# The last stage of a one-core encoder layer in two token pairs instead of four token groups at once

## The chip, the cores and the metric

The kernel runs on one core of a Trainium2 chip. Its metric is the time on the device in microseconds (us). Engines are named as the profile names them: PE (TensorE, with PEld for its weight loads), DVE (VectorE), ACT (ScalarE), POOL (GpSimd), SP (SyncE); a "q" behind a name is the engine's instruction queue, from which DMAs are issued. PSUM is the memory that PE writes, in banks of 128 x 512 float32; SBUF is the memory of everything else.

## What is computed

One encoder layer on 512 tokens of width 1024: three gated token mixers, a layer norm, a mixture of 16 experts in which each expert chooses 64 tokens, and a second layer norm. The change touches only the last expert and the second norm:

```python
def expert_choice_ffn(x, w_router, w_gate_up, w_down):
    B, T, D = x.shape
    cap = EC_CAPACITY_FACTOR * T // N_EXPERTS          # 2 * 512 // 16 = 64
    ...
    gate, idx = lax.top_k(jnp.swapaxes(aff, 1, 2), cap)
    xs = x[bidx, idx]
    h = jnp.einsum('becd,edf->becf', xs, w_gate_up)
    hg, hu = jnp.split(h, 2, axis=-1)
    ye = jnp.einsum('becf,efd->becd', jax.nn.silu(hg) * hu, w_down)
    ye = ye * gate[..., None].astype(ye.dtype)
    return jnp.zeros_like(x).at[bidx, idx].add(ye)

    ffn = expert_choice_ffn(x, w_router[l], w_gate_up[l], w_down[l])
    x = layer_norm(DN_ALPHA * x + ffn, ln2_g[l], ln2_b[l])
```

The layer norm takes mean and variance over the 1024 columns of a token, and gives (x - mean) / sqrt(var + 1e-5) * g + b.

## The kernel before, in words

**Experts.** The weights of the 16 experts stream through a ring of SBUF tiles on SP's queue (`ring`, issues at L829, some 2 MB or 1 MB a transfer). For each expert e, `gate_up` (L1312) makes two products, `act_h` the activation, `h_transpose` (L1330, copied by DVE at L1335) the transposed h, and `down` (L1347) the product with the down weights, y, 64 tokens x 1024 columns. `down` then splits y into a rounded high part and a remainder: `hi_lo`, a cast on ACT (L97) and a subtraction on DVE (L98). Two experts share one such pair of tiles (yh, yl), 128 rows. A product with a one-hot matrix GT (128 rows to 128 tokens, `g[:, m]`) scatters them back to tokens; high part and remainder are two matmuls in the rounded type fp32r. The sum over the experts, with the residual, is kept in SBUF as ACC, in four groups of 128 tokens, m = 0 to 3; mp is a pair of groups (0, 1 or 2, 3).

**The order of the work** is that in which the code is written; each engine runs its instructions in that order, and semaphores between engines are put in by the tile framework from the tiles that instructions read and write. PSUM tiles come from banks named by letters: `PB("S", ...)` takes the bank S, and has to wait until the tile that had it is done with. "mm" is a set of banks that rotate.

**The last stage** is `last_down`, called behind `down(14)`. The 1024 output columns of expert 15 are worked in four quarters q of 256 columns, since its weights come in that order, 1 MB for one quarter:

- `preload(q)` (L1443) puts ACC's columns of quarter q, which `split_acc` has split into high part and remainder, into PSUM by an identity matmul, one bank for each pair, so that the additions can accumulate onto them. Quarter 1 is preloaded earlier; quarter 2 is preloaded between the first two products, quarter 3 behind addition 2. Quarter 0 has none: DVE adds it to ACC (L1514).
- `product(q)` (L1467): 16 fp32 matmuls of expert 15's h with the weights of the quarter (in the profile 32, as each fp32 matmul is two). The output is 64 tokens x 256 columns, put as two halves of 128 columns (o = 0 on partitions 0 to 63, o = 1 on 64 to 127). All four quarters write one PSUM bank, the tile `yq`, in columns of their own.
- `split(q)`: `hi_lo` for each half, on ACT and DVE (L97, L98, 64 x 128).
- `add(q)` (L1480): eight fp32r matmuls, four groups by (yh, yl).
- statistics: `bn_stats` on DVE, for each group and quarter (L1484, L1516), and `bn_aggr` for each group at the end (L1538).
- `scaled(q)`: ACT copies the sums from PSUM to ACC (L1492), POOL multiplies them by g of the norm (L1488). The last quarter is done by DVE in one step, from PSUM (L1497).

**The norm.** g·(x - mean)·r + b, with r = 1/sqrt(var + eps), is formed as x·g·r plus a product of rank 13. `ch` (128 tokens x 4 groups x 13) holds, for each token, 1, -mean, 1/r and -mean·r in high parts and remainders; its rows come from a chain of small operations: ACT's root (L1540), DVE L1541 to L1548 and L1551 to L1553, POOL L1549 and L1550. r itself is y: a reciprocal and a Newton step. `ch` is transposed on PE for each group (rowT, L1558), copied to SBUF by ACT (`rows`, L1560), and multiplied with the rows of g and b (`low_rank`, L1566). Two matmuls of the identity (L1562) stand between transposes and low ranks. For the columns 0 to 511 (h = 0) `put` (L1504) brings x·g into PSUM by an identity matmul, the low rank is added there, and ACT scales by r (L1573). For the columns 512 to 1023 (h = 1) the low rank stands alone in PSUM, and DVE makes x·g·r plus low rank (L1571). Each (m, h) is then stored, 256 KB: six stores on SP's queue, and those of (2, 0) and (3, 0) on ACT's (L1574).

Of the kernel before, what the change touches and what calls it, by code (L numbers as in the profile page):

```python
# [69 lines left out]
def layer_kernel(ctx: ExitStack, tc: tile.TileContext, xt, xn, first0, wu, bgate, rpb, gains, wrt,  # L70
# [696 lines left out]
    class Attn:  # L767
# [4 lines left out]
        def add(self, us):  # L772
            self.units += us
# [228 lines left out]
    eps = small([P, 1], "eps", bufs=1)  # L1002
    nc.gpsimd.memset(eps, LN_EPS)
    warm_s = small([P, 1], "warm_s", bufs=1)
# [433 lines left out]
    def preload(q, banks):  # L1438
        t = ACCP.pop(q)
        r = [PB(b, f"xq{q}{mp}", (P, 2, 256)) if isinstance(b, str) else b for mp, b in enumerate(banks)]  # L1440
        for mp in range(2):
            for n in range(2):
                nc.tensor.matmul(r[mp], ident_r, t[:, n, 2 * mp:2 * mp + 2], start=(n == 0), stop=False)  # L1443
        return r

    def last_down(g2, xq, spare):
# [8 lines left out]
        cols = quarters  # L1455
# [15 lines left out]
        def split(q):  # L1471
            b = cols[q].start
            for o in range(2):
                c = slice(b + o * P, b + (o + 1) * P)
                hi_lo(yh[r, c], yl[r, c], part(q, o))

        def add(q):
            order = [(n, m) for m in range(NT) for n in range(2)] if q == 0 else [(n, m) for n in range(2) for m in range(NT)]
            for n, m in order:
                nc.tensor.matmul(xq[q][m // 2][:, m % 2], g[:, m], (yh, yl)[n][:, cols[q]], start=(q == 0 and n == 0),  # L1480
                                 stop=(n == 1 and (q == 0 or m % 2 == 1)))

        def stats(q, m):
            nc.vector.bn_stats(st[:, m, q], xq[q][m // 2][:, m % 2])  # L1484

        def times_g(mp, q):
            x = ACC[mp][:, :, cols[q]]
            nc.gpsimd.tensor_tensor(x, x, g2[:, None, cols[q]].to_broadcast([P, 2, 256]), op=ALU.mult)  # L1488

        def scaled(q):  # L1490
            for mp in range(2):
                nc.scalar.copy(ACC[mp][:, :, cols[q]], xq[q][mp])  # L1492
                times_g(mp, q)

        def scaled_last(q):
            for mp in range(2):
                nc.vector.tensor_tensor(ACC[mp][:, :, cols[q]], xq[q][mp],  # L1497
                                        g2[:, None, cols[q]].to_broadcast([P, 2, 256]), op=ALU.mult)
# [6 lines left out]

        product(0)
        split(0)
        xq[2] = preload(2, (spare.rearrange("p (a b) -> p a b", a=2), "Y"))
        product(1)
        split(1)  # L1510
        add(0)
        for mp in range(2):
            x = ACC[mp][:, :, cols[0]]
            nc.vector.tensor_tensor(x, x, xq[0][mp], op=ALU.add)  # L1514
            for m in (2 * mp, 2 * mp + 1):
                nc.vector.bn_stats(st[:, m, 0], acc_of(m)[:, cols[0]])  # L1516
            times_g(mp, 0)
        product(2)
        split(2)
        add(1)  # L1520
        for m in range(NT):
            stats(1, m)
        scaled(1)
        product(3)
        add(2)
        xq[3] = preload(3, ("T", "S"))
        split(3)
        for m in range(NT):
            stats(2, m)
        add(3)  # L1530
        scaled(2)
        put(0, "mm")
        put(1, "mm")
        put(2, "S")
        put(3, "T")
        for m in range(NT):
            stats(3, m)
            nc.vector.bn_aggr(mv[:, m], st[:, m])  # L1538
        mean, var = mv[:, :, 0], mv[:, :, 1]
        nc.scalar.activation(sg, var, AF.Sqrt, bias=eps)  # L1540
        nc.vector.tensor_scalar(hv, var, LN_EPS, -0.5, op0=ALU.add, op1=ALU.mult)  # L1541
        nc.vector.tensor_scalar(ch[:, :, 3:12:8], mean[:, :, None].to_broadcast([P, NT, 2]), -1.0, None, op0=ALU.mult)
        nc.vector.scalar_tensor_tensor(ch[:, :, 5], mean, -1.0, ch[:, :, 3].bitcast(F32), op0=ALU.mult, op1=ALU.subtract)
        nc.vector.reciprocal(y, sg)
        nc.vector.tensor_tensor(a, y, y, op=ALU.mult)
        nc.vector.tensor_tensor(a, a, hv, op=ALU.mult)
        nc.vector.scalar_tensor_tensor(y, a, 1.5, y, op0=ALU.add, op1=ALU.mult)
        nc.vector.scalar_tensor_tensor(sg, hv, -2.0, y, op0=ALU.mult, op1=ALU.mult)  # L1548
        nc.gpsimd.tensor_copy(ch[:, :, 4:13:8], sg[:, :, None].to_broadcast([P, NT, 2]))  # L1549
# [7 lines left out]
        for m in range(NT):  # L1557
            nc.tensor.transpose(tp[:13, m], ch[:, m].bitcast(F32), ident)  # L1558
# [245 lines left out]
```

## Time and profile before

| | |
|---|---|
| median of 3 runs | 966.16 us (965.75 to 966.56) |
| profiled execution | 966.82 us, span of the profile 965.0 us |
| busy share of the span | PE 98%, PEld 63%, DVE 47%, ACT 29%, POOL 9% |
| last weight transfers | end near 942 us |
| last products of expert 14 | 932.95 to 934.89 us |
| products of expert 15 | start at 935.55, 938.81, 942.07 and 945.89 us |
| root (ACT) | 953.20 us |
| first store issued | 957.43 us |

Times inside the execution are counted from the start of the span. A row of the timeline reads: start, length (both us), engine, line, operation, tile written <- tiles read, shapes, count, and in brackets how long the engine had stood idle and what ended that. A row of the chain of waits reads: start, length, what. In the stretches, each engine's busy time is followed by its count of instructions; then come the clock that PE was granted (1.00 is full speed), the busy share of the DMA engines, and GB/s. In the groups of the page, the numbers behind the bar are the busy time of the group in us and the mean of one instruction in ns. Busy shares of PE include waiting inside a pipelined group, and ends of matmuls are modelled.

### The profile page before, as it was taken

How to read it: one execution, taken by the hardware profiler on the slowest of the kernel's cores; microseconds unless marked ns; L12 is line 12 of the kernel's file. 1: busy time of each engine (PE TensorE's matmuls, PEld its weight loads, DVE VectorE, ACT ScalarE, POOL GpSimd, SP SyncE). 2: the span in 40 equal slices, each digit the busy share in tenths (PEclk: the TensorE clock that was granted, in tenths of full speed). 3: DMA queues.
4: the chain of work that ended last, by engine and by line, in shares of the span. 5: the costliest groups of instructions: out<-in, count | busy, mean ns of one | idle time of the engine just before them, and what ended most of it. 6: DMA issues, size and time to landing. Idle time of an engine off the chain costs nothing.

```text
span 965.0 us, 12910 instructions
## 1 busy us (share of the span) xinstructions
PE 942.6 (98%) x5262; PEld 608.4 (63%) x5262; DVE 453.4 (47%) x851; ACT 276.5 (29%) x539; POOL 84.2 (9%) x98
## 2 busy tenths in 40 slices
PE   9999999999999999999999999999999999998996
PEld 9899878888888888887885333433344333432344
DVE  6347668874376566237454122653322223231426
ACT  6334454543444454223242111100010000100123
POOL 0002303000112231000023000000000000000003
PEclk9999999999999999999999999999999999999998
DMA  9311111111433322564919999999999999999992
GB/s 361 114 67 67 66 66 44 66 58 54 115 91 106 99 83 87 218 266 192 393 43 387 430 418 431 428 432 429 431 429 431 430 431 431 430 430 432 427 410 91
DMA packets 39192, 251.17 MB, mean 260 GB/s; under 512 B 13007, under 2 KB 13391, under 8 KB 24926
## 3 DMA queue, kind: packets, MB, share of 16 engines
q1 hardware_dynamic: 38414, 249.74, 63.8%
q8 instruction: 41, 0.67, 0.3%
q10 hardware_dynamic: 720, 0.62, 0.2%
q14 instruction: 17, 0.14, 0.0%
HBM read 247.46 MB, written 2.10 MB: 259 GB/s over the span
## 4 chain that ended last, share of the span: by engine, by line
PE 79%; DMA 10%; DVE 6%; ACT 2%; issue 2%; POOL 1%; ACTq 0%; DVEq 0%; POOLq 0%; SPq 0%
DMA w<-in_wx 10%; PE g L1312 10%; PE u L1312 9%; PE y L1347 8%; PE gate L282 4%; PE gate L284 4%; PE gate L283 4%; PE gy L670 2%; PE ga L1272 2%; PE pr L282 2%; PE nqk L284 2%; PE nqk L282 2%; PE nqk L283 2%; PE gt L657 1%; PE pr L283 1%
## 5 line engine op out<-in xcount | busy, mean ns | idle before, releaser
L1312 PE MATMUL g<-w,xs 128*64 128x512 f32 x512 | 135.0, 606 | 2.9 <-DMA w<-in_wx 2.9
L1312 PE MATMUL u<-w,xs 128*64 128x512 f32 x512 | 131.6, 592 | 0.0
L1347 PE MATMUL y<-w,hT 128*64 128x512 f32 x480 | 106.6, 594 | 3.3 <-DMA w<-in_wx 2.6
L98 DVE TENSOR_TENSOR y<-y,y 64x512 fp32r<-64x512 f32 x30 | 20.7, 689 | 134.4 <-ACT y L97 134.4
L1312 PEld LDWEIGHTS u<-w,xs 128*64 128x64 f32 x512 | 36.8, 137 | 73.1 <-issue 72.3
L97 ACT CAST y<-y 64x512 fp32r<-64x512 f32 x30 | 17.4, 580 | 224.8 <-PE y L1347 213.5
L98 DVE TENSOR_TENSOR los<-raw_twin,whi 128x1024 fp32r<-128x1024 f32 x42 | 53.4, 1272 | 58.2 <-ACT whi L97 58.0
L1347 PEld LDWEIGHTS y<-w,hT 128*64 128x64 f32 x480 | 33.8, 137 | 72.0 <-issue 64.7
L284 PE MATMUL gate<-xh,los 128*128 128x512 f32 x192 | 74.8, 390 | 0.0
L1312 PEld LDWEIGHTS g<-w,xs 128*64 128x64 f32 x512 | 30.7, 136 | 53.9 <-issue 44.8
L282 PE MATMUL gate<-xh,whi 128*128 128x512 f32 x144 | 57.2, 397 | 0.0
L283 PE MATMUL gate<-xl,whi 128*128 128x512 f32 x144 | 56.1, 390 | 0.0
L1419 DVE TENSOR_TENSOR acc<-acc,cb 128x512 f32<-128x512 f32 x56 | 35.6, 684 | 37.8 <-PE cb L1417 37.8
L97 ACT CAST whi<-raw_twin 128x1024 fp32r<-128x1024 f32 x42 | 44.0, 1049 | 8.2 <-PE wo L1110 4.3
L1488 POOL TENSOR_TENSOR acc<-acc,ln2g 128x512 f32<-128x512 f32 x6 | 7.6, 1276 | 430.1 <-DVE l2s L1516 428.1
L284 PEld LDWEIGHTS gate<-xh,los 128*128 128x128 f32 x192 | 36.0, 188 | 7.7
L98 DVE TENSOR_TENSOR los<-raw_twin,los 128x1024 fp32r<-128x1024 f32 x20 | 25.0, 1249 | 27.0 <-ACT los L97 26.9
L646 ACT ACTIVATE att_twin<-gs,nm 128x512 f32<-128x512 f32 x32 | 21.7, 684 | 49.0 <-DVE nm L645 49.0
L1322 ACT ACTIVATE tg<-g 128x512 f32<-128x512 f32 x16 | 9.5, 597 | 89.2 <-PE g L1312 89.2
L1335 DVE COPY hT<-ht 128x512 f32<-128x512 f32 x15 | 10.4, 691 | 44.4 <-PE ht L1330 44.4
L282 PEld LDWEIGHTS gate<-xh,whi 128*128 128x128 f32 x144 | 27.0, 188 | 6.5 <-issue 1.2
L283 PEld LDWEIGHTS gate<-xl,whi 128*128 128x128 f32 x144 | 27.1, 188 | 5.3
(436 smaller groups left out, 1863.5 us busy)
## 6 DMA issues: line engine op xcount, KB each, us to landing
w<-in_wx SPq DMA_DIRECT2D x83, 2048.0 KB
raw_twin<-in_wu SPq DMA_DIRECT2D x65, 512.0 KB
w<-in_wx SPq DMA_DIRECT2D x26, 1024.0 KB
raw<-in_wu SPq DMA_DIRECT2D x8, 512.0 KB
xr<-in_xt SPq DMA_DIRECT2D x4, 512.0 KB
macc<-in_xn SPq DMA_DIRECT2D x2, 1024.0 KB
first<-in_first SPq DMA_DIRECT2D x4, 384.0 KB
bf<-in_rpb SPq DMA_DIRECT2D x64, 24.0 KB
```

The source lines that it names most:

```text
L97: nc.scalar.copy(hi, src)
L98: nc.vector.tensor_tensor(lo, src, hi.bitcast(F32), op=ALU.subtract)
L282: nc.tensor.matmul(acc, w_h, rh[:, k], start=(k == 0), stop=False)
L283: nc.tensor.matmul(acc, w_h, rl[:, k], start=False, stop=False)
L284: nc.tensor.matmul(acc, w_l, rh[:, k], start=False, stop=(k == nk - 1))
L646: nc.scalar.activation(self.p[:, h], self.s[h], AF.Exp, bias=nm[:, h:h + 1], accum_out=self.sm[:, h:h + 1])
L670: nc.tensor.matmul(self.y[h * 64:h * 64 + 64, :P], ST["vg"][:, kc, kvh * 64:kvh * 64 + 64], self.pt[:, h, kc], start=(kc == 0), stop=(kc = ...
L1272: nc.tensor.matmul(g, XH[:, m, c], oh[:, m, sl], start=(m == 0), stop=False)
L1312: nc.tensor.matmul(GU[e][b][hf * 64:hf * 64 + 64], xs, w[b][:, hf * 512:hf * 512 + 512], start=(k == 0), stop=(k == KD - 1))
L1335: nc.vector.tensor_copy(t, tp)
L1347: nc.tensor.matmul(y[o * 64:o * 64 + 64], hT[:, c, hf * 64:hf * 64 + 64], w[j][:, o * 512:(o + 1) * 512], start=(k == 0 and j == 0), stop= ...
L1419: nc.vector.tensor_tensor(a, a, cb, op=ALU.add)
```

## The change

It touches the last stage and the end of `down(14)` only.

- **Products into two banks.** Quarter q goes into bank S (`yqa`) or Y (`yqb`) by q % 2; of quarter 3, half o = 0 goes into the one and o = 1 into the other. `add(0)` stands behind `product(1)`, `add(1)` directly behind `product(2)`, each in the order of the groups.
- **Quarter 3 isn't split.** ACT and DVE copy one half each, as fp32, into a tile `Y3`, and the addition is one fp32 matmul for each group instead of two fp32r ones. Expert 14's rows of that quarter are copied into `Y3` as well.
- **y14** is first copied from PSUM to SBUF by ACT (three copies), then split by DVE with a copy and a subtraction (columns 0 to 767 only).
- **Preloads.** The one of quarter 2 goes into `down(14)`: pair 0 (into bank T) ahead of its last four matmul groups (k = 3), pair 1 behind them. The one of quarter 3 stands behind `add(1)`. The addition of quarter 2 is made for the groups 2, 3 ahead of `product(3)` and for 0, 1 behind it.
- **Two pairs at the end.** Statistics, root, chain, `ch` on POOL, transposes, rows, low ranks and outputs are made first for the groups 0, 1, then for 2, 3. Each step of the chain stands there twice, with two columns instead of four. hv (-0.5·(var + eps)) and -mean are made by ACT, behind the root, instead of DVE; the constant -0.5·eps is one POOL memset more.
- **The last quarter's multiplication by g** moves from DVE to ACT (copy) and POOL (multiplication), one for each pair; POOL has eight such multiplications instead of six.
- **Matmuls of the identity** ahead of transposes: none for the first pair, six for the second.
- **Stores** all on SP's queue, in the order (0,0), (1,0), (0,1), (1,1), (2,0), (2,1), (3,0), (3,1), as (m, h).

The core of the diff (unchanged helpers left out):

```diff
@@ down
-    def down(e, mid=lambda: None):
+    Y3 = []
+
+    def down(e, ahead=lambda k: None):
...
         for k in range(4):
-            if k == 2:
-                mid()
+            ahead(k)
...
+        if e == NEXP - 2:
+            Y3.append(R("oh", [P, 256], "y3"))
+            t = [R("t", [P, 512], f"y14{o}", bufs=2)[r, :512 - 256 * o] for o in range(2)]
+            for o in range(2):
+                nc.scalar.copy(t[o], y[o * 64:o * 64 + 64, :512 - 256 * o])
+            nc.scalar.copy(Y3[0][r], y[64:, 256:])
+            for o in range(2):
+                c = slice(o * 512, 512 + 256 * o)
+                nc.vector.tensor_copy(yh[r, c], t[o])
+                nc.vector.tensor_tensor(yl[r, c], t[o], yh[r, c].bitcast(F32), op=ALU.subtract)
+            return
@@ last_down
-        yq = PB("S", "yq")
+        bank = [PB("S", "yqa"), PB("Y", "yqb")]
         def part(q, o):
-            return yq[64 * o:64 * o + 64, q * P:(q + 1) * P]
+            return bank[o if q == 3 else q % 2][64 * o:64 * o + 64, q * P:(q + 1) * P]
...
         def split(q):
...
+                if q < 3:
+                    hi_lo(yh[r, c], yl[r, c], part(q, o))
+                else:
+                    (nc.vector.tensor_copy if o else nc.scalar.copy)(Y3[0][r, o * P:o * P + P], part(q, o))
...
+        def add(q, ms):
+            for m in ms:
+                dst = xq[q][m // 2][:, m % 2]
+                if q == 3:
+                    nc.tensor.matmul(dst, g[:, m].bitcast(F32), Y3[0], start=False, stop=(m % 2 == 1))
+                    continue
...
+        def root(mp):
+            p = slice(2 * mp, 2 * mp + 2)
+            nc.scalar.activation(sg[:, p], mv[:, p, 1], AF.Sqrt, bias=eps)
+            nc.scalar.activation(hv[:, p], mv[:, p, 1], AF.Identity, bias=heps, scale=-0.5)
+            nc.scalar.activation(ch[:, p, 3:12:8], mv[:, p, 0, None].to_broadcast([P, 2, 2]), AF.Copy, scale=-1.0)
+
+        def chain(mp):
...
+            nc.vector.reciprocal(y[:, p], sg[:, p])
+            nc.vector.scalar_tensor_tensor(a[:, p], y[:, p], 1.0, y[:, p], op0=ALU.mult, op1=ALU.mult)
+            nc.vector.scalar_tensor_tensor(a[:, p], a[:, p], 1.0, hv[:, p], op0=ALU.mult, op1=ALU.mult)
+            nc.vector.scalar_tensor_tensor(y[:, p], a[:, p], 1.5, y[:, p], op0=ALU.add, op1=ALU.mult)
+            nc.vector.scalar_tensor_tensor(sg[:, p], hv[:, p], -2.0, y[:, p], op0=ALU.mult, op1=ALU.mult)
+            nc.gpsimd.tensor_copy(c[:, :, 4:13:8], two(sg[:, p]))
+            nc.gpsimd.tensor_tensor(c[:, :, 6], sg[:, p], c[:, :, 4].bitcast(F32), op=ALU.subtract)
...
+        def rows_T(mp):
+            tp = PB("Y", f"rowT{mp}", (P, 2, P))
+            for _ in range(6 * mp):
+                nc.tensor.matmul(tp[:, 0], ident, ident, start=True, stop=True)
...
+        product(0)
+        split(0)
+        product(1)
+        add(0, range(NT))
+        split(1)
...
+        product(2)
+        add(1, range(NT))
+        split(2)
+        xq[3] = [preload(3, mp, b) for mp, b in enumerate("ST")]
...
+        add(2, (2, 3))
+        product(3)
+        stats(2, 1)
+        scaled(2, 1)
+        times_g(2, 1)
+        add(2, (0, 1))
+        split(3)
+        stats(2, 0)
+        scaled(2, 0)
+        times_g(2, 0)
+        add(3, range(NT))
+        stats(3, 0)
+        root(0)
+        put(0, "mm")
+        put(1, "mm")
+        put(2, "mm")
+        chain(0)
+        scaled(3, 0)
+        scaled(3, 1)
+        rows_T(0)
+        put(3, "T")
+        for mp in range(2):
+            times_g(3, mp)
+        stats(3, 1)
+        root(1)
+        for m in range(2):
+            tl[m, 1] = PB("S", f"lr{m}")
+            low_rank(m, 0)
+            low_rank(m, 1)
+            finish(m, 0)
+        chain(1)
+        rows_T(1)
+        for m in range(2):
+            finish(m, 1)
+        for m in range(2, NT):
+            tl[m, 1] = PB("ST"[m - 2], f"lr{m}")
             low_rank(m, 0)
             low_rank(m, 1)
             finish(m, 0)
             finish(m, 1)
```

More of the change, by code (lines that the diff above doesn't have):

```diff
@@ L1436, in split_acc, with preload, last_down @@
             hi_lo(t[:, 0, m2], t[:, 1, m2], ACC[mp][:, :, quarters[q]])
[L1438 to L1443, printed above, removed]
+    def preload(q, mp, bank):
+        t = ACCP[q]
+        r = PB(bank, f"xq{q}{mp}", (P, 2, 256)) if isinstance(bank, str) else bank
+        for n in range(2):
+            nc.tensor.matmul(r, ident_r, t[:, n, 2 * mp:2 * mp + 2], start=(n == 0), stop=False)
         return r
-    def last_down(g2, xq, spare):
+    def last_down(g2, xq):
         e = NEXP - 1
@@ L1471, in split @@
         def split(q):
-            b = cols[q].start
+            b = quarters[q].start
             for o in range(2):
                 c = slice(b + o * P, b + (o + 1) * P)
[L1475 to L1481, printed above, removed]
@@ L1504, in put @@
             nc.tensor.matmul(tl[m, 0], ident, acc_of(m)[:, 0:512], start=True, stop=False)
[L1506 to L1545, printed above, removed]
@@ new lines, in low_rank @@
+        def low_rank(m, h):
+            nc.tensor.matmul(tl[m, h], rows[m // 2][:13, m % 2], gb[:13, h * 512:h * 512 + 512], start=bool(h), stop=True)
+        rows = {}
+        def rows_T(mp):
+            tp = PB("Y", f"rowT{mp}", (P, 2, P))
+            for _ in range(6 * mp):
+                nc.tensor.matmul(tp[:, 0], ident, ident, start=True, stop=True)
+            for i in range(2):
+                nc.tensor.transpose(tp[:13, i], ch[:, 2 * mp + i].bitcast(F32), ident)
+            rows[mp] = R("t", [P, 2, P], f"rows{mp}", F32R, bufs=2)
+            nc.scalar.copy(rows[mp][:13], tp[:13])
@@ L1651, in layer_kernel @@
             gate_up(e, (4, 5))
-            x1q = preload(1, ("mm", "mm"))
+            x1q = [preload(1, mp, "mm") for mp in range(2)]
             gate_up(e, (6, 7))
```

83 lines of the change are left out of this document (43 added, 40 removed).

## The prediction

> **What bounds the kernel now.** I read the page first, then the chain that ended last from 900 us on, then the timeline and the stretches of the tail. The page's slices show the DMA engines busy throughout the experts, at some 430 GB/s until the last slice:
>
> ```profile
> GB/s 361 114 67 67 66 66 44 66 58 54 115 91 106 99 83 87 218 266 192 393 43 387 430 418 431 428 432 429 431 429 431 430 431 431 430 430 432 427 410 91
> ```
>
> The chain (start, length, what) says what follows the weights:
>
> ```profile
> 915.86 19.56 DMA w<-in_wx
> ...
> 935.55 1.98 PE yq L1467 x32
> ...
> 945.89 1.97 PE yq L1467 x32
> ...
> 950.69 0.44 DVE l2s L1484
> ...
> 955.16 0.60 PE rowT L1558 x4
> ...
> 958.29 0.74 DVE acc L1571
> ```
>
> Up to 935.42 (915.86 + 19.56) the last chain is weight transfers, and the change moves none of them. What it can change is the tail: 935.4 to 965.0, 29.6 us. There the chain goes from products to additions (until 950.69), statistics, roots and transposes (955.16), low ranks and outputs. Then come the stores; here are the row of SP's queue, the other two with the size of each, and three of the stretches (last two columns: DMA share and GB/s):
>
> ```profile
> 957.43 3.47 SPq L1574 DMA_DIRECT2D out<-acc  x6
> ```
> ```profile
> out<-acc ACTq DMA_DIRECT2D x2, 256.0 KB
> ```
> ```profile
> 958.00:959.00 1.00, 0.26 (x2) 0.00 (x0) 1.00 (x3) 0.57 (x2) 0.00 (x0) 1.00 0.73 283
> ...
> 962.00:963.00 1.00, 0.00 (x0) 0.00 (x0) 0.00 (x0) 0.00 (x0) 0.00 (x0) 0.50 1.06 408
> 963.00:964.00 1.00, 0.00 (x0) 0.00 (x0) 0.00 (x0) 0.00 (x0) 0.00 (x0) 0.50 0.49 186
> ```
>
> 256 KB at 408 GB/s are 0.643 us, so eight take 5.14. Bytes run until about 963.46 (186/408 of the last stretch), hence from 958.32: 0.9 after the first issue. The span ends 1.5 after the last byte. So before: 957.43 + 0.9 + 5.14 + 1.5 = 965.0. The outputs are made faster than they are stored (issues are done by 960.9), and **the first store's issue sets the end**. That is what splitting into pairs can shift: once half of the stores have gone early, the fifth issue sets it, with four stores behind it instead of eight.
>
> **The change, step by step.** *Products.* The last four blocks of weights are 1 MB each:
>
> ```profile
> w<-in_wx SPq DMA_DIRECT2D x26, 1024.0 KB
> ```
>
> One is 2.43 us at 431 GB/s, so estimated landings are 935.42, 937.85, 940.28 and 942.71. The products of before lag behind them, because all four write one PSUM bank and each waits for the split of the one before:
>
> ```profile
> 940.71 1.21 PE L1480 MATMUL xq<-y,GT 128*128 128x256 f32 x8
> 942.07 1.97 PE L1467 MATMUL yq<-w,hT 128*64 128x128 f32 x32 [0.15 <-DVE y L98]
> ...
> 945.89 1.97 PE L1467 MATMUL yq<-w,hT 128*64 128x128 f32 x32 [0.70 <-DVE y L98]
> ...
> 948.85 1.09 PE L1443 MATMUL xq<-accp,ident_r 128*128 128x512 f32 x4
> 949.78 1.11 PE L1480 MATMUL xq<-y,GT 128*128 128x256 f32 x8
> 950.73 3.60 PE L1504 MATMUL fin<-acc,ident 128*128 128x512 f32 x8
> ```
>
> After: two banks in turn. The preloads of quarter 2 go ahead of the last products of expert 14 and behind them, into the gap in front of 935.55; this moves those last products 0.4 later (two preload matmuls, half of L1443's four) into the same gap. y14's copies on ACT and subtractions on DVE stay two passes of the same tiles, beside product 0, with about 0.2 us to spare; if that is gone, the first addition is late by the excess. Then PE: product 0 at 935.9 (0.35 later, behind preload 2), product 1 at the landing, 937.9; from there it is PE's own sum. One product is 1.95, an addition 0.98, a preload of one quarter 0.95 (L1443's four): product 1 to 939.8, addition 0 to 940.8, product 2 to 942.8, addition 1 to 943.8, preload 3 to 944.8, half of addition 2 to 945.3, product 3 to 947.25, the other half to 947.75. So product 3 starts only 0.5 earlier (945.89 before), but preload 3 (0.95) and half of addition 2 no longer stand behind it.
>
> *Addition 3* becomes four fp32 matmuls of 128x256 instead of eight rounded ones. The tail has no such row. L1504 is fp32: eight passes of 128x512, 0.43 each, two for one matmul. Half the columns: 0.215, so eight passes are 1.72, an estimate, which takes addition 3 to 949.5 (before: 950.7). The bounds are L1562's passes of 128x128, four in 0.61 (0.86 for eight), and L1504's own (3.44). I take the middle, proportional to the columns: a pass of 128 and one of 512 stand as 1 to 4.
>
> *First pair.* Its halves of the additions are ready at 948.7. The rows of before for one item each:
>
> ```profile
> 952.50 0.37 DVE L1484 BATCH_NORM_STATS2 l2s<-xq 128x6 f32<-128x256 f32 x1
> 952.90 0.26 DVE L1538 BATCH_NORM_AGGREGATE l2mv<-l2s 128x2 f32<-128x24 f32 x1
> ...
> 953.57 0.17 DVE L1544 RECIPROCAL l2y<-l2v 128x4 f32<-128x4 f32 x1
> ...
> 954.36 0.16 DVE L1548 SCALAR_TENSOR_TENSOR l2v<-l2h,l2y 128x4 f32<-128x4 f32 x1
> ```
> ```profile
> 950.74 0.59 ACT L1492 COPY acc<-xq 128x512 f32<-128x512 f32 x1
> 953.20 0.30 ACT L1540 ACTIVATE l2v<-l2mv,eps 128x4 f32<-128x4 f32 x1 [1.88 <-DVE l2mv L1538]
> 955.80 0.63 ACT L1560 CAST rows<-rowT 13x128 fp32r<-13x128 f32 x2 [2.30 <-PE rowT L1558]
> 956.72 1.85 ACT L1573 ACTIVATE acc<-fin,l2y 128x512 f32<-128x512 f32 x3 [0.29 <-issue]
> ```
> ```profile
> 950.74 2.49 POOL L1488 TENSOR_TENSOR acc<-acc,ln2g 128x512 f32<-128x512 f32 x2 [0.84 <-ACT acc L1492]
> 954.59 0.20 POOL L1549 CAST ch<-l2v 128x8 fp32r<-128x8 f32 x1 [1.35 <-DVE l2m L1551]
> 954.87 0.22 POOL L1550 TENSOR_TENSOR ch<-l2v,ch 128x4 fp32r<-128x4 f32 x1
> ```
> ```profile
> 955.60 0.61 PE L1562 MATMUL lr<-ident 128*128 128x128 f32 x4
> ...
> 957.87 0.39 PE L1566 MATMUL lr<-gb,rows 13*128 13x512 f32 x1
> ```
>
> Two statistics with their aggregates, some 0.7 each behind each other: 950.25. Root 0.30; the chain's five dependent DVE steps at the 0.2 step of before (953.57 to 954.5), 1.0: 951.6; POOL's two, 0.2 each: 952.1; two transposes, then one copy of rows (0.37, between the two of L1560): 953.1; low ranks from 953.3, of which the first output needs two. ACT's outputs (0.6 each) at 953.8 and 954.4 give the first issues: **954.55 and 955.15**, against 957.43.
>
> *Second pair.* Its statistics follow the first chain on DVE: 951.95 to 953.35; root to 953.7. The change adds a meeting here. The last quarter's multiplication by g leaves DVE (L1497) for POOL: ACT copies (0.59), POOL multiplies, 1.25 each, behind the first pair's two ch steps: 952.1 to 953.35 and to 954.6. The chain's steps from 953.7 read two SBUF operands on DVE while POOL multiplies. What the trace shows of such a meeting:
>
> ```profile
> 157.06 1.31 POOL L415 TENSOR_TENSOR ropevg<-mkvzs,consts 128x512 f32<-128x512 f32 x1
> ...
> 159.78 1.70 POOL L418 TENSOR_TENSOR ropevg<-ropevg,ropesq 128x512 f32<-128x512 f32 x1
> ...
> 161.45 2.49 POOL L418 TENSOR_TENSOR ropevg<-ropevg,ropesq 128x512 f32<-128x512 f32 x1
> ```
> ```profile
> 160.83 1.75 DVE L98 TENSOR_TENSOR los<-raw_twin,los 128x1024 fp32r<-128x1024 f32 x1
> ```
> ```profile
> L98 DVE TENSOR_TENSOR los<-raw_twin,los 128x1024 fp32r<-128x1024 f32 x20 | 25.0, 1249 | 27.0 <-ACT los L97 26.9
> ```
>
> DVE's 1.25 became 1.75 and ended 1.1 after POOL's end (161.48): it waited. So I let the second chain's first product wait from 953.9 to 954.6, 0.6 in all; the bounds are none and the whole multiplication (1.25). The rest of the chain ends 955.25, POOL's two ch steps 955.8. The six warm matmuls (twelve passes of 0.108, 1.3 us) run from 954.3 to 955.6 under that wait; at twice the price they would cost 1.0. Transposes 955.9, rows to 956.8, low ranks, ACT's output 957.3 to 957.95: **fifth issue 958.0**. DVE makes outputs (0,1) and (1,1) from 955.6 to 957.0, behind its chain and behind POOL's multiplication; issues 956.4 and 957.05.
>
> [...]
>
> *Other edits.* -mean and hv on ACT, behind its root (each at most L1540's 0.30): hidden by the reciprocal and the wait; without that cover 0.2 for the second pair. All stores on SP's queue: six issues of before took 3.47, under 0.6 each, less than the 0.643 that a store moves, so nothing. The doubled small steps are counted above; the third `put` moves to another bank, with no wait.
>
> *Sum.* The first four stores are through by 957.05 + 0.9 + 0.64 = 958.6, ahead of the fifth's start (958.9). End: 958.0 + 0.9 + 4 x 0.643 + 1.5 = 963.0 against 965.0. The profiled execution's time is 966.82, 0.66 above the median; 966.82 - 2.05 = 964.77, which is **964.1** as a median (966.16 - 2.05).
>
> **Rivals.** (1) *No wait at the port*: a product of 128x2 slips past POOL. For it: the reciprocal at 157.11, beside POOL's L415, took its usual 0.17. Against it: that reads one operand, these two. The fifth issue comes 0.35 earlier (then the warm matmuls set it, not the whole 0.6): 963.8. (2) *Dearer fp32 addition*, or as much delay elsewhere on the full PE: at 3.44 for 1.72 the first pair's half is 0.86 later and the whole 1.72; the `put`s, transposes and warm matmuls queued behind it on PE carry some 1.25 of that to the second pair: gain 0.8, 965.4. For it: only shapes of 128 and 512 were seen. Against it: they are proportional. (3) *Slower: POOL's last two multiplications are held up.* DVE's statistics and chains now run beside them, and the meeting can go the other way. The second chain and (0,1), (1,1) wait for their ends, so each us on one costs two: gain 2.05 - 2(d - 1.25) for a multiplication of d. It turns at d = 2.3. The multiplication at 161.45, behind the L98 above, took 2.49: 966.6. If 1.25 were stretched as the two tensor_scalars beside POOL are here (2.80 for 0.88, 3.2 times), d would be 4.0 and the time 966.16 + 3.45 = 969.6:
>
> ```profile
> 157.11 0.17 DVE L577 RECIPROCAL rc<-sm 128x2 f32<-128x2 f32 x1 [0.38 <-ACT att_twin L646]
> 157.31 2.80 DVE L579 TENSOR_SCALAR att_twin<-att_twin,rc 128x512 f32<-128x512 f32 x2
> ...
> 164.96 0.88 DVE L579 TENSOR_SCALAR att_twin<-att_twin,rc 128x512 f32<-128x512 f32 x2
> ```
>
> Against it: L98 holds 1024 elements and the chain's steps hold 4 or less, 0.16 each; and POOL's six multiplications of before run 1.25 each beside DVE's statistics from PSUM. A mild case (d = 1.7, gain 1.1) goes with rival 2. (4) *The change doesn't do what it says*: if addition 3 still waited for the first pair's work, or the fifth output came after all four of the first pair, the stores would again run in one block. PE's sum from 937.9 speaks against the first; for the second the DVE outputs (0,1) and (1,1) would have to be 0.95 later than 957.05, which the mild case of rival 3 does not reach. The gain would then be what the first store still gives up to that block, some 1: with rival 2 too.
>
> **How the numbers follow.** Chances: forecast 0.40 (964.1), no wait 0.26 (963.8), dearer addition or another delay of about one us 0.23 (965.1 to 965.4), POOL held up 0.11 (from 966.2 up). 0.2% is 1.93 us, about what a measurement of this kernel can tell from no change, and the forecast's gain of 2.05 is hardly above it: over it lie half of the forecast's cases and nearly all of the first rival's, 0.20 + 0.25, and some that gain more by steps which I priced at nothing, 0.05: faster 0.50. Below lie the other half, rival 2 and the near part of rival 3: same 0.41. Slower 0.09, the far part of rival 3. The range runs from 963.4 (963.8, less the 0.4 by which the runs shown lie off their median) to 965.7 (965.4 and 0.3): it leaves out rival 3 and little else.
>
> **What would show it.** Product 1 starting at its weights' landing near 937.9 and PE without gaps to 949.5; addition 3 at 0.43 a matmul; first issues at 954.5 and 955.2, the fifth at 958.0; the first STT of the second chain 0.6 late, ending with POOL's second multiplication; POOL's last multiplications at 1.25. It is wrong if the fifth store isn't the one that sets the end, if a multiplication on POOL takes over 2.3, or if the stores move less than 408 GB/s when outputs are still being written.

## The result, and the profile after

| | before | after |
|---|---|---|
| median, us (19 runs each) | 965.84 (965.04 to 968.28) | 964.50 (963.17 to 965.13) |
| ratio | | 0.9982, 95% interval 0.9976 to 0.9988 |
| profiled execution: time, span, us | 966.82, 965.0 | 963.93, 962.1 |

The changed kernel is faster, by 0.18% or 1.7 us (1.2 to 2.3) by the ratio, which agrees with the means of these runs; the two medians differ by 1.3. The two profiled executions differ by 2.9 us. About half of that isn't the change: the weights simply came earlier in the second one. Here is the issue of the last transfer of weights on SP's queue, before, then after:

```profile
923.16 0.33 SPq L829 DMA_DIRECT2D w<-in_wx  x1
```

```profile
921.68 0.33 SPq L829 DMA_DIRECT2D w<-in_wx  x1
```

That is 1.48 us earlier, with the same steps between the last four, to 0.01 us. It isn't owed to the change: in the kernel before with one edit behind this issue (e5 below) it comes at 921.32, earlier still. **So from here on times of other executions are shifted until this issue falls at 923.16**; "counted" marks such a time. The span after ends at 962.15 + 1.48 = 963.63 counted: 1.4 us before the 965.0 of before.

PE in the timeline of the changed kernel (start and length in us; rows as the trace has them, unshifted):

```profile
936.50 1.97 PE L1479 MATMUL yqb<-w,hT 128*64 128x128 f32 x32
938.40 1.22 PE L1499 MATMUL xq<-y,GT 128*128 128x256 f32 x8
939.54 1.97 PE L1479 MATMUL yqa<-w,hT 128*64 128x128 f32 x32
...
946.46 1.97 PE L1496 MATMUL xq<-y,GT 128*128 128x256 f32 x8
948.26 2.74 PE L1519 MATMUL fin<-acc,ident 128*128 128x512 f32 x6
951.05 0.38 PE L1553 MATMUL rowT<-ident,ch 128*13 128x128 f32 x2
...
953.35 1.60 PE L1551 MATMUL rowT<-ident 128*128 128x128 f32 x12
954.79 0.38 PE L1553 MATMUL rowT<-ident,ch 128*13 128x128 f32 x2
955.68 0.50 PE L1544 MATMUL fin<-gb,rows 13*128 13x512 f32 x1 [0.51 <-ACT rows L1555]
```

No product waits for DVE any more: the brackets "<-DVE y L98" of before are gone, and no row of PE has a bracket until the rows of the second pair. The additions end at 948.4, 949.9 counted, against 950.7. What the norm waits for is its first statistic of quarter 3, on DVE:

```profile
947.60 0.43 DVE L1504 BATCH_NORM_STATS2 l2s<-xq 128x6 f32<-128x256 f32 x1 [0.19 <-PE xq L1496]
```

That is 949.08 counted, 1.6 earlier than before (950.69, L1484 in the chain of waits). Then roots (ACT), the products of y with itself (DVE, L1532) and POOL:

```profile
948.94 0.29 ACT L1523 ACTIVATE l2v<-l2mv,eps 128x2 f32<-128x2 f32 x1 [0.92 <-DVE l2mv L1506]
...
952.16 0.29 ACT L1523 ACTIVATE l2v<-l2mv,eps 128x2 f32<-128x2 f32 x1 [0.28 <-DVE l2mv L1506]
```

```profile
949.47 0.30 DVE L1532 SCALAR_TENSOR_TENSOR l2a<-l2y 128x2 f32<-128x2 f32 x1
949.88 0.16 DVE L1533 SCALAR_TENSOR_TENSOR l2a<-l2a,l2h 128x2 f32<-128x2 f32 x1
...
952.49 0.17 DVE L1531 RECIPROCAL l2y<-l2v 128x2 f32<-128x2 f32 x1 [0.36 <-ACT l2v L1523]
952.69 0.76 DVE L1532 SCALAR_TENSOR_TENSOR l2a<-l2y 128x2 f32<-128x2 f32 x1
953.55 0.16 DVE L1533 SCALAR_TENSOR_TENSOR l2a<-l2a,l2h 128x2 f32<-128x2 f32 x1
```

```profile
944.80 4.96 POOL L1513 TENSOR_TENSOR acc<-acc,ln2g 128x512 f32<-128x512 f32 x4 [0.45 <-ACT acc L1509]
...
950.92 2.50 POOL L1513 TENSOR_TENSOR acc<-acc,ln2g 128x512 f32<-128x512 f32 x2
954.17 0.19 POOL L1536 CAST ch<-l2v 128x4 fp32r<-128x4 f32 x1 [0.74 <-DVE l2m L1538]
954.44 0.20 POOL L1537 TENSOR_TENSOR ch<-l2v,ch 128x2 fp32r<-128x2 f32 x1
```

L1532 writes 128 x 2 elements, like L1533, which takes 0.16. In the second chain it took 0.76 and ended at 953.45, with POOL's multiplication (950.92 + 2.50 = 953.42). In the first it took 0.30 and ended at 949.77, with POOL's four (944.80 + 4.96 = 949.76). The stores, the first and the fifth on their own, and three stretches (columns as before):

```profile
953.53 0.35 SPq L1563 DMA_DIRECT2D out<-acc  x1
```

```profile
956.98 0.33 SPq L1563 DMA_DIRECT2D out<-acc  x1
```

```profile
958.00:959.00 1.00, 0.00 (x0) 0.00 (x0) 0.00 (x0) 0.00 (x0) 0.00 (x0) 0.98 1.03 395
959.00:960.00 1.00, 0.00 (x0) 0.00 (x0) 0.00 (x0) 0.00 (x0) 0.00 (x0) 0.50 1.06 406
960.00:961.00 1.00, 0.00 (x0) 0.00 (x0) 0.00 (x0) 0.00 (x0) 0.00 (x0) 0.50 0.45 172
```

The first store goes out at 955.01 counted (957.43 before), the fifth at 958.46. Four stores of 0.643 us, the fifth and the three behind it, with 0.9 ahead, make 956.98 + 0.9 + 2.57 = 960.45, and the bytes end there (172/406 of the last stretch is 960.42).

### The profile page after: what moved, and what is told of

It is laid out like the page before. It is cut to its first block, busy times and chain, and to the rows that moved or that the text cites. A ratio compares the mean times of both kernels' runs of the same rounds, so it can differ in the third digit from the quotient of the medians.

```text
span 962.1 us, 12945 instructions
## 1 busy us (share of the span) xinstructions
PE 944.4 (98%) x5270; PEld 609.2 (63%) x5270; DVE 454.0 (47%) x857; ACT 278.1 (29%) x546; POOL 88.5 (9%) x103
## 4 chain that ended last, share of the span: by engine, by line
PE 84%; DMA 8%; DVE 4%; POOL 1%; ACT 1%; issue 1%; DVEq 0%; POOLq 0%; ACTq 0%; SPq 0%
PE g L1314 10%; PE u L1314 9%; PE y L1350 9%; DMA w<-in_wx 8%; PE gate L282 4%; PE gate L283 4%; PE gate L284 4%; PE pr L282 2%; PE pr L283 2%; PE pr L284 2%; PE gy L670 2%; PE ga L1274 2%; PE nqk L282 2%; PE nqk L283 2%; PE nqk L284 2%; PE gt L657 1%
## 5 line engine op out<-in xcount | busy, mean ns | idle before, releaser
L98 DVE TENSOR_TENSOR los<-raw_twin,whi 128x1024 fp32r<-128x1024 f32 x42 | 53.6, 1277 | 59.4 <-ACT whi L97 59.2
L98 DVE TENSOR_TENSOR y<-y,y 64x512 fp32r<-64x512 f32 x28 | 19.3, 689 | 129.8 <-ACT y L97 120.4
L1513 POOL TENSOR_TENSOR acc<-acc,ln2g 128x512 f32<-128x512 f32 x8 | 10.0, 1275 | 427.8 <-ACT y L97 427.3
L98 DVE TENSOR_TENSOR los<-raw_twin,los 128x1024 fp32r<-128x1024 f32 x20 | 25.0, 1248 | 26.3 <-ACT los L97 26.2
```

The costliest lines, as they stand in the source:

```text
L98: nc.vector.tensor_tensor(lo, src, hi.bitcast(F32), op=ALU.subtract)
```

## The experiments

Two theories were to be told apart. **A**: the gain is made in the front, where products no longer wait for splits, and the pairs only pass it on. **B**: the gain is made by the two pairs. Each kernel below was timed in five rounds against the kernel before; ratios have intervals of about 0.001 to either side, 0.9 us. Most of the kernels lie within that of each other, so what tells them apart is the trace, one execution of each: the issues of the first and the fifth store and the end of the span, all counted.

| kernel | ratio (95% interval) | first store | fifth store | end |
|---|---|---|---|---|
| before | 1 | 957.43 | 958.85 | 965.01 |
| changed | 0.9982 (0.9976 to 0.9988) | 955.01 | 958.46 | 963.63 |
| one bank (e1) | 0.9997 (0.9988 to 1.0006) | 956.46 | 959.91 | 965.10 |
| one norm (e2) | 0.9987 (0.9978 to 0.9996) | 956.08 | 958.22 | 963.85 |
| before, two banks (e5) | 0.9996 (0.9987 to 1.0004) | 957.06 | 958.48 | 964.64 |
| preload 2 back (e6) | 0.9988 (0.9980 to 0.9997) | 955.59 | 959.03 | 964.20 |
| quarter 3 split (e7) | 0.9988 (0.9979 to 0.9997) | 955.00 | 958.45 | 963.63 |
| no identity matmuls (e3) | 0.9985 (0.9976 to 0.9994) | 954.95 | 958.33 | 963.50 |
| g late (e9) | 0.9983 (0.9975 to 0.9992) | 955.35 | 958.80 | 963.96 |
| g late, no identity matmuls (e4) | 0.9977 (0.9968 to 0.9986) | 955.04 | 957.83 | 963.00 |
| the same, put(3) late (e10) | 0.9978 (0.9968 to 0.9987) | 954.82 | 957.79 | 962.96 |
| e4 with two queues (e11) | 0.9972 (0.9960 to 0.9984) | 954.97 | 957.76 | 962.89 |
| g on DVE, no identity matmuls (e8) | 0.9989 (0.9981 to 0.9998) | 955.34 | 959.07 | 964.25 |

In "g late" and "g on DVE" product 1 started at 938.32 counted instead of 938.0: there the weights of quarter 1 came 0.3 us later behind the last issue, and all that follows is to be read 0.3 earlier.

**One bank.**

```diff
-        bank = [PB("S", "yqa"), PB("Y", "yqb")]
+        bank = [PB("S", "yq")] * 2
```

> The changed kernel with one edit: all products of the last expert go into one PSUM bank again, as before the change; the two pairs, the order and all else stay. Times within the execution are counted from the issue of the last weight transfer. Theory A (the gain comes from the products that no longer wait for a split, so the additions end earlier; the pairs only pass it on): product 2 starts 1 us later than in the changed kernel, the end of the additions and all eight stores move by about 1.8 us, and of the gain of 1.7 us over the kernel before about 0.2 is left (966.0 if before is 966.2). Theory B (the gain comes from the two pairs, since half of the stores go out early whatever the products do): the gain stays at 1.4 us or more.

PE in the timeline of this kernel:

```profile
933.97 1.97 PE L1479 MATMUL yq<-w,hT 128*64 128x128 f32 x32
937.23 1.97 PE L1479 MATMUL yq<-w,hT 128*64 128x128 f32 x32 [1.29 <-DVE y L98]
...
940.50 1.97 PE L1479 MATMUL yq<-w,hT 128*64 128x128 f32 x32
```

The wait for the split is back, 1.29 us of idle PE. All stores come 1.45 us later than in the changed kernel, and nothing measurable is left of its gain (1.0006 to 0.9988). The pairs are all there, and the first store goes out 1 us before that of the kernel before; but the fifth goes out at 959.91, and 959.91 + 0.9 + 2.57 = 963.4 is hardly earlier than what the first store of before makes, 963.5. The first statistic of quarter 3 starts here at 948.76, 950.67 counted, which is when it does in the kernel before (950.69): where quarter 3 is ready no earlier than before, the pairs, as they are built here, gain nothing. Theory B falls.

**One norm.** Pairs undone at the norm; the core of the edit:

```diff
-            p = slice(2 * mp, 2 * mp + 2)
+            p = slice(0, 4)
...
         stats(3, 0)
+        stats(3, 1)
         root(0)
...
-        stats(3, 1)
-        root(1)
...
-        chain(1)
```

> The changed kernel with the pairs undone at the norm: statistics of all four groups first, then one root, one chain and two POOL steps of four columns; transposes of all groups behind it, no matmuls of the identity ahead of them. Products, additions, the copies of the last quarter and the order of the stores stay. Theory A: the first store goes out about 1.2 us later than in the changed kernel but the fifth at about the same time; the end is then again set by the first stores and comes 0.4 us later, so that 1.3 of the gain of 1.7 us is left. Theory B (the pairs make the gain): the gain falls to 0.3 us or less.

The end comes 0.22 us later than in the changed kernel: the pairs, as they are built in the changed kernel, are worth that much (0.4 expected). One chain instead of two brings the fifth store forward (958.22), but the first back to 956.08, and now the first sets the end again: 956.08 + 0.9 + 8 x 0.643 = 962.1, where the changed kernel has 961.9. This kernel has neither the identity matmuls nor a POOL multiplication beside its chain; against the version of the pairs without these two ("g late, no identity matmuls" below, end at 963.00) it is 0.85 us later.

**Two banks alone**, in the kernel before:

```diff
-        yq = PB("S", "yq")
+        yq = [PB("S", "yqa"), PB("T", "yqb")]
...
-            return yq[64 * o:64 * o + 64, q * P:(q + 1) * P]
+            return yq[q % 2][64 * o:64 * o + 64, q * P:(q + 1) * P]
```

> The kernel before with one edit: its products go into two PSUM banks in turn (quarters 0 and 2 into one, 1 and 3 into the other); nothing else of the change, one norm for all groups. Times counted from the issue of the last weight transfer. Theory A (two banks help only together with the moved preload: here the preload of quarter 2 still stands between products 0 and 1 and takes 1.3 us there, as long as the wait for the split that it used to fill): product 1 starts at 938.8 as before, product 2 0.3 us and product 3 some 1 us earlier, the first store 0.75 us earlier, gain 0.7 us. Rival (the bank is the whole of it): product 1 starts at 938.0, gain 1.4 us or more.

Product 1 started at 938.57 counted, 0.24 earlier, product 3 1.24 earlier, but the first store only 0.37, and the time can't be told from that of before. Theory A named the preload rightly, but the gain is half of what it expected (0.4 for 0.7). The rest is in this kernel's chain of waits, which has changed engines (times unshifted):

```profile
939.97 0.70 DVE acc L1514
940.67 0.02 issue
940.69 0.75 DVE l2s L1516 x2
941.44 0.60 DVE acc L1514
942.04 0.02 issue
942.07 0.75 DVE l2s L1516 x2
942.82 0.03 issue
942.85 0.29 DVE y L98
```

Here split 2 (L98, at 942.85) stands behind 2.8 us of additions and statistics of quarter 0 on DVE, and DVE sets the pace from there.

**Preload 2 back** between products 0 and 1, two banks kept:

```diff
-        elif k == 3:
-            xqs[2] = [preload(2, 0, "T")]
...
-    xqs[2].append(preload(2, 1, spare.rearrange("p (a b) -> p a b", a=2)))
...
         split(0)
+        xq[2] = [preload(2, 0, "T"), preload(2, 1, spare.rearrange("p (a b) -> p a b", a=2))]
         product(1)
```

> The changed kernel with one edit: the preload of quarter 2 goes back from the end of expert 14's products to its place between products 0 and 1 of expert 15; the two banks stay. Theory A: product 0 starts 0.35 us earlier, product 1 0.6 us or more later, and the fifth store with it: 0.6 us slower than the changed kernel, of the gain of 1.7 us 1.1 left. Rival (the preload is hidden there as before): no change.

As theory A has it: product 1 at 938.54, fifth store 0.57 later, end 0.57 later. In the kernel before the preload cost nothing at this place, since PE was waiting there for the split. With the wait gone it is 0.6 us.

**Quarter 3 split again:**

```diff
-                if q < 3:
-                    hi_lo(yh[r, c], yl[r, c], part(q, o))
-                else:
-                    (nc.vector.tensor_copy if o else nc.scalar.copy)(Y3[0][r, o * P:o * P + P], part(q, o))
+                hi_lo(yh[r, c], yl[r, c], part(q, o))
...
-                if q == 3:
-                    nc.tensor.matmul(dst, g[:, m].bitcast(F32), Y3[0], start=False, stop=(m % 2 == 1))
-                    continue
```

> The changed kernel with the last quarter split into high part and remainder again: eight fp32r matmuls for addition 3 in place of four fp32 ones, y14 split over all its columns, four more short operations on ACT and DVE. Theory A (what PE saves, 0.8 us, the longer split of product 3 gives back, 1.2 us of casts and subtractions behind each other against 0.66 us of additions beside them): the additions end within 0.2 us of the changed kernel's, the time is the same. Rival 1 (the fp32 addition is a cost on the full PE): 0.5 to 0.8 us faster than the changed kernel. Rival 2 (the unsplit quarter is a gain): 0.5 us slower.

Every store within 0.02 us of the changed kernel's. This part of the change is worth nothing. That PE's longer addition and the shorter split cancel is the explanation that was expected; the stores show only the sum.

**No identity matmuls** ahead of the second transposes:

```diff
-            for _ in range(6 * mp):
-                nc.tensor.matmul(tp[:, 0], ident, ident, start=True, stop=True)
```

> The changed kernel without the six matmuls of the identity ahead of the second pair's transposes. Theory A: they lie under the second chain's wait, and the transposes follow POOL's last step: within 0.1 us of the changed kernel, in the trace the fifth store 0.0 to 0.1 us earlier. Rival: they keep TensorE's clock up over a gap of 1.4 us, and without them the clock granted in the profile falls below 1.00 there and the four low ranks behind take twice their 0.24 us: fifth store 0.5 to 1 us later.

The fifth store comes 0.13 earlier, but 0.06 of that is there at the first store already (product 1 started 0.09 earlier, with its weights); the matmuls themselves cost 0.07. The reason stands in the changed kernel's trace: there the transposes (954.79) stand behind the last passes of the identity, not behind POOL (954.44 + 0.20). Here PE is idle for 1.3 us, and its clock stays at 1.00 over that gap (PE in the timeline of this kernel, and the stretches from the gap on):

```profile
954.58 0.38 PE L1551 MATMUL rowT<-ident,ch 128*13 128x128 f32 x2 [1.31 <-POOL ch L1537]
...
955.80 0.39 PE L1544 MATMUL lr<-gb,rows 13*128 13x512 f32 x1
```

```profile
954.00:955.00 1.00, 0.38 (x2) 0.12 (x2) 0.96 (x5) 0.00 (x0) 0.40 (x2) 1.00 0.79 305
955.00:956.00 1.00, 0.54 (x2) 0.48 (x3) 0.77 (x2) 0.36 (x1) 0.00 (x0) 1.00 0.60 231
956.00:957.00 1.00, 0.66 (x3) 0.18 (x1) 0.70 (x2) 0.95 (x2) 0.00 (x0) 0.93 1.01 391
```

The low ranks take 0.39 as before, so in this execution the rival falls. It wasn't far off, and one execution doesn't settle it: the mean clock is 1.00 in the stretch from 955, 0.93 in that from 956 and 0.50 in that from 957, so by estimate it went from 1.00 to 0.50 at about 956.86, 0.2 behind the last low rank (956.27 + 0.39). In "put(3) late" below, also without the identity matmuls, it fell while low ranks still ran (its stretch, and PE in the timeline):

```profile
956.00:957.00 1.00, 1.00 (x4) 0.54 (x3) 0.37 (x2) 0.68 (x1) 0.00 (x0) 0.61 0.96 371
```

```profile
956.37 0.62 PE L1544 MATMUL fin<-gb,rows 13*128 13x512 f32 x1
956.79 0.62 PE L1544 MATMUL lr<-gb,rows 13*128 13x512 f32 x1
```

0.62 for 0.39, though no store came later for it there. Whether the identity matmuls hold the clock up in other executions stays open.

**g late**: POOL's last multiplication behind the second chain, with and without the identity matmuls.

```diff
-        for mp in range(2):
-            times_g(3, mp)
+        times_g(3, 0)
         stats(3, 1)
...
         chain(1)
+        times_g(3, 1)
         rows_T(1)
```

> The changed kernel without the six matmuls of the identity, and with POOL's last multiplication by g (quarter 3, groups 2 and 3) moved behind the two POOL steps of the second chain, so that it no longer stands beside that chain. Theory A (the second chain's first product waits at a port for POOL's multiplication): that product takes 0.16 us instead of 0.76, the second pair's rows come 0.6 us earlier, the fifth store 0.5 us earlier, and the time is 0.5 us under the changed kernel's (a gain of 2.2 us over the kernel before). Rival (the product waits for something else, as for the constants that ACT makes): it still takes 0.7 us, and the time doesn't change.

> The changed kernel with POOL's last multiplication moved behind the second chain's POOL steps, and the six matmuls of the identity kept: the other half of the edit made before. Theory A: the chain's first product takes 0.16 us again, but the transposes now follow the twelve passes of the identity on PE instead of POOL; of the 0.63 us that both edits together took from the fifth store, about half is left (0.2 to 0.4 us earlier than in the changed kernel), gain over the kernel before 1.9 to 2.1 us. Rival (the matmuls of the identity cost nothing): the whole 0.6 us.

In both the chain's first product is short (DVE, kernel without the identity matmuls):

```profile
952.55 0.16 DVE L1532 SCALAR_TENSOR_TENSOR l2a<-l2y 128x2 f32<-128x2 f32 x1
952.81 0.16 DVE L1533 SCALAR_TENSOR_TENSOR l2a<-l2a,l2h 128x2 f32<-128x2 f32 x1
```

0.16 for 0.76, so it was POOL's multiplication that it waited for; that it waits at a port isn't shown. What this is worth hangs on PE. Without the identity matmuls the fifth store comes 0.63 earlier than in the changed kernel, and so does the end. With them, nothing is gained: from first to fifth store it is 3.45 us, as in the changed kernel (958.46 - 955.01). The transposes then wait for the passes of the identity alone:

```profile
953.43 1.60 PE L1551 MATMUL rowT<-ident 128*128 128x128 f32 x12
954.88 0.38 PE L1553 MATMUL rowT<-ident,ch 128*13 128x128 f32 x2
```

while POOL's last step for them is done by 954.13 (kernel g late, POOL):

```profile
953.93 0.20 POOL L1537 TENSOR_TENSOR ch<-l2v,ch 128x2 fp32r<-128x2 f32 x1
```

Half of the 0.63 was expected there. The transposes wait for POOL and for the passes of the identity, and the two end so close together that taking one away gives 0.07 or nothing, both together 0.63.

**put(3) late**, in addition: `put(3, "T")` from ahead of the first low ranks to ahead of the second transposes.

> The kernel with POOL's last multiplication late and without the matmuls of the identity, and put(3) moved from ahead of the first pair's low ranks to ahead of the second pair's transposes. Theory A (the fifth store sets the end): the first two stores go out 0.3 us earlier, the fifth stays, and the time stays at that of the version without this edit (0.9977 of the kernel before). Rival (the first store still sets the end): 0.3 us faster.

The first store is 0.22 earlier, the fifth 0.04, the end 0.04, the ratio the same: theory A, the fifth store sets the end.

**Two queues**: "g late, no identity matmuls", with

```diff
-            nc.sync.dma_start(out[:, m, h * 512:h * 512 + 512], x)
+            (nc.scalar if h == 0 and m > 1 else nc.sync).dma_start(out[:, m, h * 512:h * 512 + 512], x)
```

> The kernel with POOL's last multiplication late and without the matmuls of the identity, and with the stores of (2,0) and (3,0) on ACT's queue again, as before the change. In all runs so far with eight stores on SP's queue the span ends 1.22 us behind the last landing of a store, in those with two on ACT's 1.04. Theory A (the end of the program is 0.18 us longer with SP's queue alone): the last landing stays where it is, counted from the last weight transfer, the span ends 0.2 us earlier, ratio to the kernel before 0.9975. Rival 1 (it is the order of landings that makes the difference, not the queue): no change. Rival 2 (the issue on ACT holds up its own outputs): the store of (3,0) comes 0.4 us later and the end 0.1 us or more later.

The last landing stays (0.02 later), and from it to the span's end it is 1.10 instead of 1.23 us: in sign theory A, in size two thirds. That it is the order of the landings and not the queue (rival 1) isn't excluded by this kernel alone, as its order of issues changed too; but the kernel before and e5 have 1.04 and 1.02 with (3,1) last, as the changed kernel has it with 1.23. It is the fastest version measured, 0.9972 of the kernel before; against the same without this edit (0.9977) the times alone don't tell.

**g on DVE**: the last quarter's multiplication back on DVE, from PSUM, behind the second chain; the identity matmuls are left out here too.

```diff
-        scaled(3, 0)
-        scaled(3, 1)
...
-        for mp in range(2):
-            times_g(3, mp)
...
-        for m in range(2):
-            finish(m, 1)
+        for mp in range(2):
+            nc.vector.tensor_tensor(ACC[mp][:, :, quarters[3]], xq[3][mp],
+                                    g2[:, None, quarters[3]].to_broadcast([P, 2, 256]), op=ALU.mult)
+            for m in range(2 - 2 * mp):
+                finish(m, 1)
```

> The changed kernel without the six matmuls of the identity, and with the last quarter's multiplication by g on DVE again, from PSUM in one step for each pair behind the second chain, in place of ACT's copy and POOL's multiplication. Theory A: the second chain's first product takes 0.16 us in place of 0.76 and its rows come 0.6 us earlier, but DVE now has 1.28 us of multiplications ahead of its outputs: (0,1) and (1,1) come 0.2 us later than in the changed kernel, (2,0) stands behind them in the stores' queue, and the time is within 0.3 us of the changed kernel's, on the slower side. Rival (the port's wait is all that counts): 0.5 us faster than the changed kernel.

The first product takes 0.16, the fifth store comes 0.3 later than in the changed kernel once the late weights are taken off (959.07 - 0.33): theory A. Moving this multiplication to POOL was no loss, though it brings the wait, since on DVE it stands ahead of the outputs.

## Why the prediction was right

964.1 was forecast with a range from 963.4 to 965.7; by the ratio it is 964.4 on the scale of the runs shown then. The gain, 2.05 by the sum, is 1.7 by the runs and 1.4 by the two traces, counted. Step by step, in counted times:

| step | forecast | measured |
|---|---|---|
| product 1, product 3 | 937.9, 945.3 | 937.98, 945.45 |
| additions end | 949.5 | 949.9 |
| first root, first transposes | 950.25, 952.1 | 950.42, 952.53 |
| first store | 954.55 | 955.01 |
| end of POOL's last multiplication | 954.6 | 954.9 |
| second transposes | 955.9 | 956.27 |
| fifth store | 958.0 | 958.46 |
| end | 963.0 | 963.63 |

- **What bounds.** That the first store sets the end of before, and the fifth that of after, held; the formula (issue + 0.9 + stores left x 0.643) gives the bytes' end of both.
- **Products and additions.** PE without gaps, as forecast; the sum was 0.15 short by product 3. Addition 3: eight passes in 1.82 on the chain's count (948.42 - 946.60), so 0.23 a pass against the estimate of 0.215; neither bound came near. Rival 2 falls. Whether this addition is cheap or dear on PE, e7 shows that it is no cost to the kernel.
- **The wait for POOL.** Right in the second chain: 0.60, ended by POOL (0.76 for 0.16). Rival 1 falls. The 0.6 was an estimate from L98 beside L418 (1.75 for 1.25); that it is a wait at a port, as the rival's name has it, no run shows: the runs show that it ends with POOL's multiplication, and that it is gone (0.16) where that stands later (e4, e9). *But the first chain waits too*, 0.14 (0.30 for 0.16), for the four multiplications ahead of it; the prediction priced it only where the change moves a multiplication.
- **The order of POOL's multiplications**, rival 3: all eight took 1.25 each. DVE waited, POOL didn't. It falls.
- **Under that wait** the six identity matmuls were to end 0.2 ahead of POOL. POOL came 0.3 later than forecast, and they began 0.5 later, behind the first pair's late low ranks; so they ended last, a cost of 0.07 (e3). That rival 1 would have been worth 0.35 "then the warm matmuls set it" was too much: e9 says nothing at all.
- **All stores on SP's queue "so nothing".** This is the step that failed outright: 0.19 us. From the last landing of a store to the end of the span it is 1.04 us before, 1.02 with two banks alone and 1.10 in e11, all with two stores on ACT's queue; in the ten other kernels, all on SP's, 1.22 or 1.23. My 1.5 behind the last byte was taken over unasked.

The shortfall of 0.65 us in the traces is thus 0.46 at the fifth store (0.15 from the products, about 0.1 each from the addition and the first chain's wait, the rest in the last steps) and 0.19 behind it. Why it is smaller in the runs, 1.7 for 1.4, stays open; the interval of the runs holds both. The forecast of over 0.2% had one case in two, and the 0.18% lies just on the other side of that line.

Rival 4, stores in one block all the same, didn't arise. What the prediction didn't ask is which part makes the gain; its sum runs front and pairs together, and they don't simply add. The front without the pairs keeps all but 0.2 us of the gain (e2), the pairs without the front, as they are built, gain nothing (e1). The 0.2 is small because the pairs pay here for POOL's multiplication and the identity matmuls beside the second chain; without these two they are worth 0.85 (e4 against e2). Of the front, two banks alone give 0.4 (e5) and the moved preload is worth 0.6 once the banks are there (e6).

## What to carry to other kernels

Before a wait is taken away, look at what stands in the gap that it leaves: a preload, a statistic or a multiplication that was free there becomes the next bound, and has to be moved in the same change. Where outputs are made faster than they are stored, write the end as the largest of "issue of store k, plus all stores from k on"; an edit counts only if it moves the store that sets this. Splitting the work in two pays only as far as nothing new is put beside the second half: here the split was worth 0.2 us with a POOL multiplication and filler matmuls beside it, and 0.85 without. Where two waits end almost together, test them together: here either edit alone gave 0.07 us or nothing, and both 0.63.

## What the runs showed of the hardware that was not expected

- A DVE product of 128 x 2 elements, both inputs from one SBUF tile, took 0.76 and 0.30 us in place of 0.16 beside POOL's multiplications of 128 x 512, and ended with them: at 953.45 beside 953.42, and at 949.77 beside 949.76 (forecast for the second chain, not for the first). The reciprocal ahead of it, with one input, took 0.17 in the second chain, beside the same multiplication. Why the one waited and the other didn't isn't shown.
- In three executions TensorE's granted clock fell near the end at three distances from the last low rank. In e3 it stayed at 1.00 over a gap of 1.31 us, and then fell by estimate 0.2 us behind the last low rank. In the changed kernel the last low rank ends at 956.87 and the clock goes to 0.50 at about 958.96 (estimated from the means of 0.98 in the stretch from 958 and 0.50 in that from 959), 2.1 us later. In "put(3) late" it fell at about 956.22 (estimated from the mean of 0.61 in the stretch from 956), while low ranks ran. What sets the time of the fall isn't shown.
- The end of the program took 0.1 to 0.2 us more in the runs with the last stores all on SP's queue (1.22 or 1.23 us behind the last landing, against 1.02 to 1.10). The cause wasn't looked for.
